# Four changes to the opening of a hybrid attention layer: load order, halved first weights, in-place low parts, deferred stores and rotary splits

## The chip, the cores and the metric

The kernel runs on one core of a Trainium2 chip. A core has five engines that this text speaks of: TensorE (PE in the profile; PEld is its weight load) multiplies matrices, VectorE (DVE) and ScalarE (ACT) work elementwise, GpSimd (POOL) does the same more slowly, and SyncE (SP) here issues every transfer, in one queue. Each engine works through its own list of instructions in order; between engines stand semaphores. The metric is device time in microseconds (us), lower is better.

## The reference

One layer of a decoder: 16 learned meta tokens and 2048 tokens x of width 1024, normalised by RMS and a gain, go through one large projection, then through two attentions side by side, stick-breaking attention with 8 heads and sliding-window attention with 16 query heads, 2 key heads, rotary positions and a sink. Both are gated, projected, merged and added to x.

```python
xn = rms_norm(h, norm_gain[l])
proj = xn @ w_in[l]
sb_q, sb_k, sb_v, sw_q, sw_k, sw_v, sb_z, sw_z, g_sb, g_sw = jnp.split(proj, offsets, axis=-1)
o_sb = stick_breaking_attention(sb_q, sb_k, sb_v, valid)      # heads of 64, no rope
q, k = rope(sw_q, pos), rope(sw_k, pos)
o_sw = sliding_window_sink_attention(q, k, sw_v, attn_sinks[l], valid)
y_sb = (o_sb * jax.nn.silu(sb_z)) @ w_branch_sb[l]
y_sw = (o_sw * jax.nn.silu(sw_z)) @ w_branch_swa[l]
merged = jax.nn.sigmoid(g_sb) * y_sb + jax.nn.sigmoid(g_sw) * y_sw
h = h + merged @ w_out[l]
```

The reshapes to heads are left out here. The result is normalised once more.

## The kernel before

Every product of float32 matrices is made of three matmuls. An operand is split into a high part h (rounded to the multiplier's format) and a low part l = operand - h, and h·h, l·h and h·l are summed in one PSUM bank (`gemm`, L404 to L406). A *tile* here is one such product of 128 output columns with a *group* of 512 tokens: 8 steps over the 1024 inputs, 24 matmuls. There are four groups; a half of the work takes two of them, the first half groups 2 and 3 (g0 and g1 below).

A weight block of 1024 x 128 is loaded (`load`), split by `weights` and `split` (L104: the cast to h on ScalarE or GpSimd, the difference on VectorE or GpSimd, as the flags `hsplit` and `vsplit` say), and both parts are stored to memory, since the second half loads them again. In the opening these stores are not issued at once but collected in `put_off`. Weight parts have three buffers, raw blocks two. Temporaries of 128 x 512 come from one ring of seven buffers (`tmp`): whoever asks for one waits until the last reader of its former content is done, and that reader may be a transfer.

The opening (L900 to L1036) works on unnormalised x, so that TensorE need not wait for the norm: x times gain is split into `xh`/`xl` (`unscaled`, L911 and L912), three products per group are made (stick-breaking keys and queries of the first two head pairs: `ts[0]` keys, `ts[1]` queries, `ts[2]` keys), and their sums are scaled by 1/rms afterwards (`scaled`, L934). Meanwhile ScalarE squares the rows of x for the norms, `rb0` and `rb1` spread the scales, and `normal` (L377 to L380) makes the normalised x of each group, with ScalarE and VectorE working on two of its eight tiles in turn. What is done with a sum stands in `use`: for keys and queries `evac_split` (L113, L114) makes two parts in two new temporaries, and four transfers store them (`sb_k`, `sb_q`).

After it the first half's sliding-window part begins (L1055): the key, value and first query block with g0 (`wk`, `wv`, `wq`), the same key and value block with g1, then the second query block, then the stick-breaking values, where attention sets in as a side stream woven into the projections. For rotary positions (`rope`, L595) ScalarE copies four quarters crosswise, VectorE makes two products with cos and sin tables, GpSimd adds; the sum is split at once into keys (`put_k`, L610 and L612: four casts, four differences) or queries (L657, L658). Small work after a tile (transposing values to rows, meta keys) is queued in `pending`, `soon`, `late` and is run inside a later tile (`lagged`, after its second, fourth, sixth step), so that it stands between matmuls on TensorE. The meta keys of the two stick-breaking blocks go through memory: `ms` is stored to `msd` (L1018), and `later` in `sb_k` loads and transposes it, queued by way of `held`. The buffers `ms` are two.

The order of TensorE is written out by hand everywhere; that of ScalarE and SyncE in the opening too, that of VectorE from there to the value tile of g1 (`hand.close()`). Elsewhere a planner orders the instructions by a simulated timeline and so also decides which buffer is free first.

Of the kernel before, what the change touches and what calls it, by code (L numbers as in the profile page):

```python
# [44 lines left out]
def tile_kernel(ctx, tc, x, xt, meta, metat, gain, w_in, w_sb, w_sw, w_out, sinks, fgain,  # L45
# [18 lines left out]

    A.preload_act_table_set("natural_log_exp_and_others")
    ident = cp.tile([P, P], F32, name="ident")
    DMA(ident, ident_c)
    gn = cp.tile([P, KT], F32, name="gn")
    DMA(gn, gain.rearrange("o (k p) -> p (o k)", p=P))
    sel = cp.tile([P, 2, P], I32, name="sel")  # L70
    skb = cp.tile([P, 16], F32, name="skb")

# [88 lines left out]
        DMA(raw, w[c0 // P])  # L161
        return raw

    def weights(c0, w=w_in, raw=None):
# [265 lines left out]
    def col_tile(w, g, use, first=False, bank="g", mbank="zm"):  # L430
# [4 lines left out]
        use(g, acc, None if pm is None else meta_sum(pm))  # L435
        yield 0.65

    def sb_k(p):
        def use(g, acc, ms):
            h, l = tmp(F32R), tmp(F32R)  # L440
            evac_split(h, l, acc)
            for i, t in enumerate((h, l)):
                DMA(kd[p][g][i][:, :GT], t)
            if ms is not None:
                def later():
                    if p < 2:
                        t = tp.tile([NM, P], F32, tag="ms", name="ms", bufs=2)
                        DMA(t, msd[p])
                    mc = meta_cols(t if p < 2 else ms, "t" if p < 2 else "zm")
                    h, l = tmp(F32R)[:, :NM], tmp(F32R)[:, :NM]  # L450
                    A.copy(h, mc)
                    V.tensor_tensor(l, mc, f32(h), op=ALU.subtract)
                    for i, t in enumerate((h, l)):
                        DMA(kd[p][3][i][:, GT:], t)
                pending.append(later)
        return weights(C_SBK + p * P), use, True

    def sb_q(p):
        def use(g, acc, ms):
            h, l = tmp(F32R), tmp(F32R)  # L460
# [108 lines left out]
    def lagged(gen):  # L569

        for n, c in enumerate(gen):
            yield c
            if n in (2, 4, 6):
                flush({2: soon, 4: late, 6: pending}[n])


    def window(half, groups, sp):
        kk = sp.tile([P, 4, 9 * P], F32R, name="kk")
# [38 lines left out]
        def sw_k():  # L617
            def use(g, acc, ms):
                n = g - groups[0]
                t = tmp()  # L620
                rope(acc, ct[:, cols(n)], sn[:, cols(n)], t, tmp(), 1.0)
                put_k(t, n * GT, GT)
                if ms is not None:
                    def later():
                        t, u = (tmp()[:, :NM] for _ in range(2))
# [22 lines left out]
        def sw_q(p):  # L648
            def use(g, acc, ms):
# [4 lines left out]
                for a in range(2):  # L654
                    r = slice(64 * a, 64 * a + 64)
                    o = slice(64 - 64 * a, 128 - 64 * a)
                    A.copy(q[r, a, :], t[r])  # L657
                    V.tensor_tensor(q[o, a, :], t[r], f32(q[r, a, :]), op=ALU.subtract)  # L658
                qs[p, g] = q, clock[0] + QW
            return weights(C_SWQ + p * P), use, False  # L660

# [240 lines left out]
    with (tc.tile_pool(name="start", bufs=1, side="left") as bp,  # L902
# [39 lines left out]
        ssq0, ssq1 = sums(), sums()  # L942
        for t in (ssq0, ssq1):
            V.memset(t, 0.0)
        ts = [sbt[0]()]
        x_tiles(("u", g0), 1)
        for k in range(KT):
            raws.append(bp.tile([P, GT], F32, tag="raw0", name="raw0", bufs=KT))
            unscaled(g0, k, raws[k])
        ts.append(sbt[2]())  # L950
        ssm = squares(meta, NM, 1)
        ts.append(sbt[1]())
        products(g0, 0, "g")
# [61 lines left out]
        for k in (4, 5):  # L1015
            new.append(pair[:, (k - 4) * GT:(k - 3) * GT])
            DMA(new[k], xt[g1, k])
        for n in (0, 2):  # L1018
            DMA(msd[n // 2], ms[n])
        for k, t in put_off:  # L1020
            DMA(k, t)
        del put_off[:]
        ready[C_SWQ] = weights(C_SWQ, raw=raw)
        outs[g0, 2] = scaled(g0, 2, rb0)
        for n in range(3):
            ts[n][1](g0, outs[g0, n], ms[n])
        for n in range(3):
            outs[g1, n] = scaled(g1, n, rb1)
        for k, t in put_off:
            DMA(k, t)  # L1030
        for k in range(0, KT, 2):
            in_turns(*(normal(g1, j, new[j], rb1) for j in (k, k + 1)))
            if k == 0:
                for j in (6, 7):
                    new.append(ring_x())
                    DMA(new[j], xt[g1, j])  # L1036
    put_off = None
    held = pending[:]
    del pending[:]
    for half, groups in enumerate(halves):  # L1040
        with tc.tile_pool(name=f"swa{half}", bufs=1, side="left") as sp:
# [12 lines left out]
            steps = [(s, g) for s in range(4) for g in groups]  # L1054
            if m:  # L1055
                (wk, use_k, _), (wv, use_v, _), (wq, use_q, _) = sw_k(), sw_v(), sw_q(0)
                drain(col_tile(wk, g0, use_k), col_tile(wv, g0, use_v), col_tile(wq, g0, use_q, bank="z"))
                for n in range(3):
                    ts[n][1](g1, outs[g1, n], None)
                drain(lagged(col_tile(wk, g1, use_k, True, "o", "t")))  # L1060
                meta_k = pending[:]
                del pending[:]
# [101 lines left out]
```

## Time and profile before

| what | value |
|---|---|
| time, median of 3 runs | 2207.05 us (2206.35 to 2208.54) |
| the profiled execution | 2209.05 us, its span 2207.3 us |
| TensorE busy | 2160.9 us (98%) |
| VectorE, ScalarE, GpSimd busy | 1365.7, 1013.8, 380.2 us |
| mean granted TensorE clock | 0.994 |
| bytes moved by DMA | 384.61 MB, mean 174 GB/s |

The span is from the first instruction to the last. A row of a timeline has the start, the length, the engine, the line, the operation with output and input, and in brackets how long the engine had stood idle before it and what ended that wait. A row of the waits has the total, the number of times and the longest. SPq is SyncE's issue of a transfer, not the transfer. Matmuls are pipelined, so one may be listed with 0.39 us though the next starts 0.23 us later.

### The profile page before, as it was taken

The numbers are of one execution on the slowest core, as the hardware profiler recorded it, in microseconds if no ns is written. First come the engines' busy times: TensorE is split into PE (matmuls) and PEld (weight loads), VectorE is DVE, ScalarE is ACT, GpSimd is POOL, SyncE is SP. The second block draws the span as 40 slices with busy tenths as digits, with TensorE's granted clock in tenths as the row PEclk, the third lists the DMA queues.
The fourth block names the chain that finished last, engine by engine and source line by source line (L and its number), as shares of the span: only waits on it lengthen the run. The fifth ranks groups of instructions, "written<-read, shape, count | busy, mean of one in ns | idle before, by whom it ended". The sixth has DMA issues, their size and how long they took to land.

```text
span 2207.3 us, 30283 instructions
## 1 busy us (share of the span) xinstructions
PE 2160.9 (98%) x10614; PEld 1771.3 (80%) x10614; DVE 1365.7 (62%) x2130; ACT 1013.8 (46%) x2332; POOL 380.2 (17%) x493
## 2 busy tenths in 40 slices
PE   8899999999999999999999999999999999999998
PEld 6678887788888888788887888888888888787876
DVE  6678876356555443778755888778774437453543
ACT  6566767333433323677753555555553202221121
POOL 2123342322222201233310000000000232000000
PEclk9999999999999999999999999999999999999999
DMA  9655446856455365544446433333323976467422
GB/s 335 232 175 189 172 171 210 261 182 203 161 179 180 130 232 181 172 172 151 155 135 196 120 110 113 116 99 112 115 84 129 348 271 212 147 221 271 151 91 86
DMA packets 175800, 384.61 MB, mean 174 GB/s; under 512 B 23040, under 2 KB 41216, under 8 KB 175648
## 3 DMA queue, kind: packets, MB, share of 16 engines
q1 hardware_dynamic: 175648, 382.67, 52.0%
q8 instruction: 84, 1.38, 0.3%
q14 instruction: 68, 0.56, 0.1%
HBM read 233.16 MB, written 149.37 MB: 173 GB/s over the span
## 4 chain that ended last, share of the span: by engine, by line
PE 77%; issue 2%; DVE 1%; DMA 1%; ACT 1%; POOL 0%; POOLq 0%; ACTq 0%; DVEq 0%
PE ps_g L404 12%; PE ps_g L405 12%; PE ps_g L406 12%; PE ps_o L861 6%; PE ps_z L813 6%; PE ps_t L835 5%; PE ps_o L722 1%; PE ps_z L676 1%; PE ps_g L224 1%; PE ps_g L225 1%; PE ps_z L225 1%; PE ps_g L223 1%; PE ps_z L223 1%; PE ps_z L224 1%; PE ps_t L225 1%
## 5 line engine op out<-in xcount | busy, mean ns | idle before, releaser
L404 PE MATMUL ps_g<-xh,wh 128*128 128x512 f32 x1544 | 639.2, 414 | 9.7 <-ACT xh L911 7.5
L405 PE MATMUL ps_g<-xl,wh 128*128 128x512 f32 x1544 | 609.2, 395 | 0.4 <-DVE xl L912 0.4
L406 PE MATMUL ps_g<-xh,wl 128*128 128x512 f32 x1544 | 608.9, 394 | 0.0
L824 DVE TENSOR_TENSOR_SCAN row<-row 128x512 f32<-128x512 f32 (+2 forms) x320 | 372.5, 1166 | 176.4 <-POOL row L822 105.1
L406 PEld LDWEIGHTS ps_g<-xh,wl 128*128 128x128 f32 x1544 | 291.7, 189 | 65.5
L404 PEld LDWEIGHTS ps_g<-xh,wh 128*128 128x128 f32 x1544 | 293.4, 190 | 57.3 <-ACT xh L911 7.5
L405 PEld LDWEIGHTS ps_g<-xl,wh 128*128 128x128 f32 x1544 | 293.2, 190 | 43.9 <-DVE xl L912 0.9
L817 ACT ACTIVATE row<-ps_z 128x512 f32<-128x512 f32 (+1 forms) x320 | 172.0, 538 | 276.2 <-PE ps_z L813 228.7
L114 DVE SCALAR_TENSOR_TENSOR wtl<-ps_t,wth 128x512 fp32r<-128x512 f32 (+1 forms) x320 | 189.8, 593 | 42.9 <-ACT wth L113 41.4
L113 ACT ACTIVATE wth<-ps_t 128x512 fp32r<-128x512 f32 (+1 forms) x320 | 170.4, 532 | 97.4 <-PE ps_t L835 95.8
L813 PE MATMUL ps_z<-kt,q 128*128 128x512 f32 (+3 forms) x640 | 185.0, 369 | 0.3 <-ACT row L817 0.3
L835 PE MATMUL ps_t<-ident,row 128*128 128x128 f32 x1088 | 171.6, 273 | 1.2 <-DVE row L824 1.2
L835 PEld LDWEIGHTS ps_t<-ident,row 128*128 128x128 f32 x1088 | 135.9, 140 | 37.3 <-DVE row L824 1.7
L109 POOL TENSOR_SCALAR wh<-raw 128x1024 fp32r<-128x1024 f32 (+1 forms) x71 | 75.8, 1067 | 437.6 <-PE ps_g L405 303.7
L822 POOL TENSOR_SCALAR_AFFINE_SELECT row<-row 128x128 f32<-128x128 f32 x128 | 44.1, 346 | 619.0 <-ACT row L817 584.0
L813 PEld LDWEIGHTS ps_z<-kt,q 128*128 128x128 f32 x640 | 118.7, 188 | 26.4 <-ACT row L817 0.8
L861 PE MATMUL ps_o<-wth,vc 128*128 128x512 f32 (+1 forms) x320 | 125.7, 393 | 1.3 <-DVE tmp L866 1.1
L552 ACT ACTIVATE tmp<-ps_g 128x512 f32<-128x512 f32 x112 | 67.1, 599 | 121.0 <-PE ps_g L406 113.9
L684 ACT ACTIVATE sc<-sc,nm 128x129 f32<-128x129 f32 x256 | 100.0, 392 | 37.0 <-DVE nm L682 36.4
L861 PE MATMUL ps_o<-wtl,vc 128*128 128x512 f32 (+1 forms) x320 | 116.8, 365 | 0.0
L110 POOL TENSOR_TENSOR wl<-raw,wh 128x1024 fp32r<-128x1024 f32 (+1 forms) x43 | 96.4, 2242 | 3.1
L262 ACT CAST ringl<-gt 128x512 fp32r<-128x512 f32 x32 | 19.9, 621 | 132.0 <-DVE gt L260 128.0
(293 smaller groups left out, 3457.8 us busy)
## 6 DMA issues: line engine op xcount, KB each, us to landing
raw<-in_w_in SPq DMA_DIRECT2D x58, 512.0 KB, 4.5
h_in_w_in<-wh SPq DMA_DIRECT2D x58, 512.0 KB, 3.2
l_in_w_in<-wl SPq DMA_DIRECT2D x58, 512.0 KB, 3.4
wh<-h_in_w_in SPq DMA_DIRECT2D x58, 512.0 KB, 3.7
wl<-l_in_w_in SPq DMA_DIRECT2D x58, 512.0 KB, 4.8
q<-qd SPq DMA_DIRECT2D x128, 128.0 KB, 3.4
vc<-vd SPq DMA_DIRECT2D x48, 256.0 KB, 2.7
kd<-tmp SPq DMA_DIRECT2D x32, 256.0 KB, 4.1
```

Of the source, the lines that this page charges most:

```text
L110: (V if vsplit[0] else G).tensor_tensor(l, src, f32(h), op=ALU.subtract)
L113: A.activation(h, acc, AF.Copy, scale=scale)
L114: V.scalar_tensor_tensor(l, acc, scale, f32(h), op0=ALU.mult, op1=ALU.subtract)
L404: T.matmul(acc, lhsT=wh[:, k, :], rhs=xh[g][:, k, :], start=k == 0, stop=False)
L405: T.matmul(acc, lhsT=wh[:, k, :], rhs=xl[g][:, k, :], start=False, stop=False)
L406: T.matmul(acc, lhsT=wl[:, k, :], rhs=xh[g][:, k, :], start=False, stop=k == KT - 1)
L684: A.activation(sc[:, hh, :], sc[:, hh, :], AF.Exp, bias=nm[:, hh:hh + 1], accum_out=den[:, hh:hh + 1])
L813: T.matmul(z[:, :w], lhsT=lq, rhs=kt[h][:, k0:k0 + w], start=t == 0, stop=t == 1)
L817: A.activation(r[:, :w], z[:, :w], AF.Sigmoid, scale=-1.0)
L824: V.tensor_tensor_scan(r[:, :w], r[:, :w], r[:, :w], last[j] if n else 1.0, op0=ALU.mult, op1=ALU.min)
L835: T.transpose(tr[:, j * P:(j + 1) * P], rows_of[h, g, n - (j > i), j][:, k0:k0 + P], ident)
L861: T.matmul(o[:, :n], lhsT=v, rhs=r, start=first and r is wh, stop=last and r is wl)
```

## The change

Four edits, all in the opening and the first tiles behind it.

- *Load order and halves.* The first weight block is loaded ahead of everything, the gain vector behind it, the identity behind the second weight block. The first block is split by halves (steps 0 to 3, then 4 to 7): the first half on ScalarE and VectorE, the second after the first x tile, on ScalarE and GpSimd.
- *Low parts over the sums.* While `spare` is set, `sb_k` and `sb_q` write the low part into the temporary that holds the sum.
- *Stores behind the last x.* The stores of the sliding-window weights (`put_off`: key, value and first query block, two parts each) and of `msd` are issued behind the loads of g1's last two x tiles, no longer ahead of the first group's key and query stores. The second group's sums are split and stored ahead of its normalised x, no longer among the rotary products.
- *Rotary products ahead of their splits.* For the first three tiles (`hold`), `put_k` and the query split are kept in `waiting` and run after all three ropes. `held` is queued one round later.

```diff
-    DMA(ident, ident_c)
     gn = cp.tile([P, KT], F32, name="gn")
-    DMA(gn, gain.rearrange("o (k p) -> p (o k)", p=P))
...
+    spare = [False]
+    def low(acc):
+        return acc.bitcast(F32R) if spare[0] else tmp(F32R)
...                                   # sb_k and sb_q, each
-            h, l = tmp(F32R), tmp(F32R)
+            h, l = tmp(F32R), low(acc)
...
+    waiting = []
+    def then(f):
+        if hold[0]:
+            waiting.append(f)
+        else:
+            f()
+    hold = [False]
...                                   # sw_k
-                put_k(t, n * GT, GT)
+                then(lambda: put_k(t, n * GT, GT))
...                                   # sw_q: the split becomes put_q
+                then(put_q)
...                                   # opening
+        def by_halves(wh, wl, raw):
+            a, b = slice(0, KT // 2), slice(KT // 2, KT)
+            A.copy(wh[:, a], raw[:, a])
+            V.tensor_tensor(wl[:, a], raw[:, a], f32(wh[:, a]), op=ALU.subtract)
+            def rest():
+                A.copy(wh[:, b], raw[:, b])
+                G.tensor_tensor(wl[:, b], raw[:, b], f32(wh[:, b]), op=ALU.subtract)
+            second.append(rest)
+        raw = load(C_SBK)
+        DMA(gn, gain.rearrange("o (k p) -> p (o k)", p=P))
+        ready[C_SBK] = weights(C_SBK, raw=raw, split=by_halves)
         ts = [sbt[0]()]
         x_tiles(("u", g0), 1)
         for k in range(KT):
             raws.append(bp.tile([P, GT], F32, tag="raw0", name="raw0", bufs=KT))
             unscaled(g0, k, raws[k])
+            if k == 0:
+                second[0]()
         ts.append(sbt[2]())
+        DMA(ident, ident_c)
...
-        for n in (0, 2):
-            DMA(msd[n // 2], ms[n])
-        for k, t in put_off:
-            DMA(k, t)
-        del put_off[:]
         ready[C_SWQ] = weights(C_SWQ, raw=raw)
+        spare[0] = True
         outs[g0, 2] = scaled(g0, 2, rb0)
         for n in range(3):
             ts[n][1](g0, outs[g0, n], ms[n])
         for n in range(3):
             outs[g1, n] = scaled(g1, n, rb1)
-        for k, t in put_off:
-            DMA(k, t)
+        for n in range(3):
+            ts[n][1](g1, outs[g1, n], None)
+        spare[0] = False
+        for n in (0, 2):
+            DMA(msd[n // 2], ms[n])
         for k in range(0, KT, 2):
             in_turns(*(normal(g1, j, new[j], rb1) for j in (k, k + 1)))
             if k == 0:
                 for j in (6, 7):
                     new.append(ring_x())
                     DMA(new[j], xt[g1, j])
+                for j, t in put_off:
+                    DMA(j, t)
...                                   # first half
+                hold[0] = True
                 drain(col_tile(wk, g0, use_k), col_tile(wv, g0, use_v), col_tile(wq, g0, use_q, bank="z"))
-                for n in range(3):
-                    ts[n][1](g1, outs[g1, n], None)
+                hold[0] = False
+                flush(waiting)
                 drain(lagged(col_tile(wk, g1, use_k, True, "o", "t")))
...
-                pending.extend(held)
+                pending.append(lambda: pending.extend(held))
```

More of the change, by code (lines that the diff above doesn't have):

```diff
@@ L162, in load, with weights @@
         return raw
-    def weights(c0, w=w_in, raw=None):
+    def weights(c0, w=w_in, raw=None, split=split):
         if c0 in ready:
@@ L459, in use @@
         def use(g, acc, ms):
-            h, l = tmp(F32R), tmp(F32R)
+            h, l = tmp(F32R), low(acc)
             evac_split(h, l, acc, 0.125)
@@ L653, in use, with put_q @@
                 q = sp.tile([P, 2, GT], F32R, tag="q", name="q", bufs=QB)
[L654 to L658, printed above, removed]
+                def put_q():
+                    for a in range(2):
+                        r = slice(64 * a, 64 * a + 64)
+                        o = slice(64 - 64 * a, 128 - 64 * a)
+                        A.copy(q[r, a, :], t[r])
+                        V.tensor_tensor(q[o, a, :], t[r], f32(q[r, a, :]), op=ALU.subtract)
+                then(put_q)
                 qs[p, g] = q, clock[0] + QW
@@ L944, in tile_kernel @@
             V.memset(t, 0.0)
+        second = []
+        def by_halves(wh, wl, raw):
[9 more added lines that the diff above has]
+        ready[C_SBK] = weights(C_SBK, raw=raw, split=by_halves)
         ts = [sbt[0]()]
```

## The prediction

> **What bounds the kernel now.** I read the page's shares first, then TensorE's waits over the opening, then busy time and granted clock by stretch.
>
> ```profile
> PE 2160.9 (98%) x10614; PEld 1771.3 (80%) x10614; DVE 1365.7 (62%) x2130; ACT 1013.8 (46%) x2332; POOL 380.2 (17%) x493
> ```
> ```profile
> PE ps_g L404 <- ACT xh L911: 7.5, 1, 7.5
> PE ps_zm L473 <- ACT tmp L469: 3.7, 1, 3.7
> PE ps_zm L520 <- DVE vt L114: 3.0, 2, 1.6
> PE ps_o L405 <- DVE xl L380: 2.7, 3, 2.2
> PE ps_o L404 <- ACT xh L378: 2.4, 3, 1.3
> PE ps_t L427 <- DMA ms<-msd: 1.9, 1, 1.9
> ```
> ```profile
> 47.10:112.80 65.70, 55.07 (x252) 42.45 (x249) 39.30 (x64) 31.65 (x63) 16.37 (x17) 0.92 0.66 231
> 74.68:78.09 3.41, 3.41 (x15) 2.63 (x16) 1.80 (x3) 3.33 (x6) 1.28 (x1) 0.52 0.80 261
> 95.16:98.58 3.42, 3.42 (x10) 2.65 (x9) 3.25 (x5) 3.26 (x7) 0.12 (x1) 0.52 0.73 216
> 105.41:108.82 3.41, 3.41 (x21) 2.93 (x19) 1.51 (x6) 1.11 (x4) 0.00 (x0) 0.52 0.04 5
> 112.80:160.00 47.20, 44.10 (x238) 36.51 (x238) 37.18 (x74) 32.45 (x97) 13.96 (x16) 1.00 0.57 190
> 160.00:2190.00 2030.00, 2012.48 (x9903) 1653.07 (x9902) 1249.17 (x1912) 913.82 (x2100) 343.59 (x450) 1.00 0.51 169
> ```
>
> In the last fence each row is a stretch: its length, then busy time and instructions of TensorE, its weight loads, VectorE, ScalarE and GpSimd, the granted clock, and the transfer engines' share and rate. TensorE is busy 98% of the span, and the built order of instructions differs from the old one only up to the first tiles of attention. So the change can move only what TensorE loses there: the start (7.5 us), and the stretch from 47.10 to 112.80, in which it stands idle 65.70 - 55.07 = 10.6 us and runs three times for 3.41 us at half the clock (0.52), which costs another 0.48 x 3.41 = 1.6 us each.
>
> **Part 1, the opening loads and the halves.** These rows are SyncE's issues, the first work of ScalarE and VectorE and TensorE's first wait for it, and then TensorE in full run: three matmuls, one step of a product, take 0.68 us.
>
> ```profile
> 1.71 0.58 SPq L55 DMA_DIRECT2D raw<-in_w_in  x1
> 2.33 3.99 SPq L55 DMA_DIRECT2D raw<-in_xt  x8
> 6.65 0.33 SPq L55 DMA_DIRECT2D raw<-in_w_in  x1
> 5.65 1.04 ACT L107 CAST wh<-raw 128x1024 fp32r<-128x1024 f32 x1 [3.59 <-DMA raw<-in_w_in]
> 6.73 1.22 DVE L110 TENSOR_TENSOR wl<-raw,wh 128x1024 fp32r<-128x1024 f32 x1 [4.31 <-ACT wh L107]
> 8.67 0.79 PE L405 MATMUL ps_g<-xl,wh 128*128 128x512 f32 x1 [0.37 <-DVE xl L912]
> ```
> ```profile
> 52.66 0.39 PE L404 MATMUL ps_g<-xh,wh 128*128 128x512 f32 x1
> ...
> 53.34 0.39 PE L404 MATMUL ps_g<-xh,wh 128*128 128x512 f32 x1
> ```
>
> The weights are issued first, ahead of two others, by at most the 1.71 us at which they are issued now and nearer to 0.9. The gain vector stays ahead of the first x tile, which must not land later. That tile landed at about 6.6 (the issue at 6.65 waits for it), just as the cast ended (5.65 + 1.04); so an earlier, halved cast alone gains little, and the gain is the x tile's: 0 to 0.9 us, since it still queues behind the weights and the gain's 4-byte pieces. I take 0.8 and start TensorE at 6.7. VectorE's half (1.22/2 = 0.6) now ends before x, so the second matmul no longer waits for it. Against that stand the second cast of 0.5 us, ahead of the next x tiles on ScalarE, and its difference on GpSimd, beside VectorE's own work. The first matmuls run at half rate in either case, so an earlier start is partly spent there: of 0.8 to 1.2 us I keep **0.5** (bounds: a loss of 0.5, a gain of 1.2).
>
> [...]
>
> **Part 2, what runs into the second group's first tile.** SyncE's queue, VectorE, ScalarE, and the stores' usual time to landing.
>
> ```profile
> 50.72 1.19 SPq L55 DMA_DIRECT2D l_in_w_in<-wl  x1
> 52.02 3.17 SPq L55 DMA_DIRECT2D kd<-tmp  x2
> ```
> ```profile
> 50.66 0.69 DVE L934 TENSOR_TENSOR tmp<-ps_z,rb 128x512 f32<-128x512 f32 x1
> 58.62 0.69 DVE L934 TENSOR_TENSOR tmp<-ps_o,rb 128x512 f32<-128x512 f32 x1 [7.27 <-DMA kd<-tmp]
> ...
> 63.00 1.29 DVE L380 TENSOR_TENSOR xl<-xs,xh 128x512 fp32r<-128x512 f32 x2 [1.67 <-ACT xh L378]
> ```
> ```profile
> 59.93 0.59 ACT L598 ACTIVATE tmp<-ps_g 32x512 f32<-32x512 f32 x1 [10.04 <-DMA qd<-tmp]
> ```
> ```profile
> kd<-tmp SPq DMA_DIRECT2D x8, 256.0 KB, 4.1
> ```
>
> VectorE stands 7.27 us for a temporary buffer that the store of the first group's keys holds, and that store queues behind the weights' (four of 0.5 MB, of which 50.72 is the last). Now the weights' six stores go last, and the low parts reuse the sums. The store leaves at about 48.4 (with the first high part) and lands, by its row's 4.1 us, at 52.5. Then come two sums, to 53.9. Three high parts (0.63 each) that wait for one landing each are ready by 55.6, and with the last low part (0.69) the moved products are done at 56.3. The rope copies of ScalarE follow (4 x 0.6, to 58.0). So the first pair of x tiles has its high parts at 59.2, and low parts at 59.2 and 59.9 instead of 63.7 and 64.3; each later pair takes 2.7 (four VectorE operations of 0.67), so the eighth low part stands at 68. TensorE is at that tile after three others of 8 steps from 47.10, at 63.8 - 0.5 = 63.3, and needs the eighth low part at the end of its eighth step, 7 x 0.69 + 0.2 later, at 68.3. Of the 2.7 + 2.4 = 5.1 us I give back 0.4: **-4.7** (bounds 2.5 and 5.1; the poor end is a landing of 6.6 us, from 52.02 to 58.62, as now). The last two x tiles are issued behind six stores of keys and queries, at about 60.2, and have to land by 65.3: 1.6 MB of stores from about 57 and 0.5 MB of tiles at 0.33 MB per us (261 GB/s at a share of 0.80, in the row from 74.68) end at 63.4, and a landing follows by a us or two.
>
> **Part 3, the collision of VectorE and GpSimd.** The last two x tiles' products were slow for another reason than their loads.
>
> ```profile
> 69.05 1.55 POOL L109 TENSOR_SCALAR wh<-raw 128x1024 fp32r<-128x1024 f32 x1 [14.78 <-DMA xs<-in_xt]
> 70.69 2.67 POOL L110 TENSOR_TENSOR wl<-raw,wh 128x1024 fp32r<-128x1024 f32 x1
> ```
> ```profile
> 71.06 2.84 DVE L377 SCALAR_TENSOR_TENSOR xs<-xs,gn,rb 128x512 f32<-128x512 f32 x1
> ```
>
> An operation that takes 0.7 us elsewhere took 2.84 while GpSimd split the second query weights. After the change that split uses the buffers of the key weights, so it waits until TensorE has left them and those weights' stores have landed, and stands behind both rope additions: cast at about 71, split until 75.5 to 76. TensorE asks for it at 77: a tile is 8 x 0.69 = 5.5, a meta product 16 matmuls of a quarter of the columns, by estimate 0.9, and 63.3 + 5.5 + 0.9 + 5.5 + 0.9 with the transposes is 76.6. The split then meets the key splits of VectorE (L612) instead of the x tiles. The next weights' low part (1.22, as at 6.73; the value projection's) stands behind these on VectorE, and comes at 82 to 85, where TensorE, one tile further, asks at about 83. I take **+1.0** (bounds 0 and 2.6).
>
> [...]
>
> **Part 4, rotary products, value transposes and meta keys.**
>
> ```profile
> 81.71 0.63 ACT L113 ACTIVATE tmp<-tmp 128x512 fp32r<-128x512 f32 x1
> ...
> 89.61 0.63 ACT L113 ACTIVATE tmp<-tmp 128x512 fp32r<-128x512 f32 x1 [0.95 <-DVE tmp L114]
> ...
> 93.32 0.59 ACT L469 COPY tmp<-ps_z 128x512 f32<-128x512 f32 x1 [0.77 <-DMA qd<-tmp]
> ...
> 112.91 0.17 ACT L530 COPY tmp<-ps_zm 128x16 f32<-128x16 f32 x1 [5.63 <-PE ps_zm L427]
> ```
>
> Three splits of the second group (0.63 each on ScalarE, the first at 81.71, the last at 89.61) and their waits leave the way of the copy at 93.32. After the last x tile's cast at 67.3 ScalarE has one copy (0.6), rope of q (4 x 0.6), a split (0.6), rope of k (2.4), four key casts and two q casts (0.63 each, as the splits), and then that copy, done at about 78 with small ones between; TensorE wants it in the seventh step of its tile from 76.6, at 81.5. **-3.7**, with +0.5 for the bank in which it lands, which VectorE empties only after the deferred splits. Deferring costs on: the second group's key splits, the value rows and the next rope stand behind GpSimd's addition, so the 16-column transposes of the meta keys and the product after them may wait, on a path that is quiet now: **+1.0** (0 to 2).
>
> The wait of 1.9 us for the reload of the meta keys stays. The second reload uses the first one's buffer, so it is issued only after the first transpose, and in the new order the two transposes still stand side by side; moving them one tile later hides the first load alone: 0. After it ScalarE waits 5.63 us for TensorE, so the lag of the other engines ends there, and what is won should stay won: from 160 on TensorE is 99% busy at full clock.
>
> **The sum.** Idle time and new waits: -0.5 - 4.7 - 3.7 + 0.5 + 1.0 + 1.0 = -6.4. Two of the three stretches at half clock (the first two, each right after a stall that goes) fall away: -3.2; the third stays with that 1.9 us. Six restarts after short stalls go with them; no row prices them alone, and between 0 and 0.3 us each I take 0.15: -0.9. In all **-10.5 us**. The profiled execution took 2209.05 us (its span and 1.75 around it), which gives 2198.5; the median of the runs shown, 2207.05, lies 2.0 below it, which gives 2196.5. I say 2197.5.
>
> **The rivals.** A measurement of this kernel tells 0.2%, 4.4 us.
> - *All of it.* No new wait shows, and the third half-clock stretch goes too: 2197.5 - 2.5 - 1.6 - 0.4 = 2193. For it: the new waits are of 1 us and stand on estimates. Against: GpSimd's collision is in the trace. 0.17.
> - *The temporaries still wait for stores.* Each landing takes 6.6 us instead of 4.1, and the chain of six such waits ends 3 to 4 us later; the x tiles come late by as much, and half clock with them: 2202. For it: 58.62 - 52.02. Against: 2 MB less in front. 0.15.
> - *Won and lost again.* The attention that follows is bound by ScalarE or VectorE, not by TensorE's arrival: 2207. Against: 5.63 us of ScalarE's waiting at 112.9. 0.07.
> - *Slower: the late weight stores hold GpSimd.* The second query weights need the key weights' buffers, whose stores (0.5 MB each) now go after everything else; GpSimd stands in order, with the rope of q behind it. I reckon that they land at 68. From a landing at about 74, each us later is a us of TensorE; to undo 10.5 they must land at 85, and at 90 the time is 2212. For it: 1 to 3 MB in one queue. Against: the queue moves 0.2 to 0.4 MB per us and is near empty at 105 (5 GB/s). 0.06.
>
> **How the numbers follow.** Forecast 0.55, rivals 0.17, 0.15, 0.07, 0.06. Low end 2190 (all of it, with 3 us more from the start and the clock), high end 2204 (the second rival and a bit): that leaves out the last two and little else. The likeliest case's own range is 2194 to 2201. Faster by over 0.2% means below 2202.6: 0.55 + 0.17 and most of the second rival, 0.85; within: 0.08; slower: 0.07.
>
> **What would show it.** Right: TensorE's first matmul at 6.3 to 7.0; no 7 us wait of VectorE at 51; the waits for x parts (5.1) under 1.5 in all; none for the value copy (3.7); about 1.9 still at the meta transposes; ScalarE's copy of 112.91 at 100 to 104. Wrong: a TensorE wait for the second query weights of GpSimd, for the value weights' low part, or for the keys' rope over 2 us each, or a stall at 63 to 69 as large as now.

## The result, and the profile after

The changed kernel takes 2197.55 us (median of 7 runs, 2194.74 to 2201.59), the kernel before 2207.05 us (7 runs, 2204.25 to 2211.18). The ratio is 0.9955 with a 95% interval of 0.9943 to 0.9968, so the change wins 9.5 us, 7 to 12.6 by the interval; the forecast was 2197.5. The profiled execution took 2194.74 us, its span 2193.0.

Of the changed kernel, first the row of the engines on the page, then TensorE's waits over the first 170 us.

```profile
PE 2153.9 (98%) x10614; PEld 1766.6 (81%) x10614; DVE 1368.2 (62%) x2130; ACT 1014.1 (46%) x2333; POOL 380.7 (17%) x494
```
```profile
PE ps_g L402 <- ACT xh L929: 6.9, 1, 6.9
PE ps_zm L524 <- DVE vt L112: 2.9, 2, 1.6
PE ps_zm L425 <- DVE vv L112: 2.3, 1, 2.3
PE ps_t L425 <- DMA ms<-msd: 1.7, 1, 1.7
PE ps_g L404 <- DVE wl L108: 0.6, 1, 0.6
PE ps_o L403 <- DVE xl L378: 0.2, 1, 0.2
PE ps_t L540 <- DVE tmp L509: 0.2, 1, 0.2
PE ps_o L402 <- ACT xh L376: 0.2, 1, 0.2
```

The waits for the x parts (2.7 and 2.4 before) are down to 0.4, and the 3.7 for the value copy are gone. New are 2.3 us until VectorE has made the value rows' low part (`vv`) out of the bank `zm`, and 0.6 for a weight's low part. The reload of the meta keys keeps its wait, 1.7.

A good place to compare the two is the transpose of meta sums that stands right behind the two reloaded ones; behind it the order of TensorE is the same. Call it the mark. Before and after:

```profile
112.64 0.23 PE L427 MATMUL ps_zm<-ident,ms 16*128 16x16 f32 x1
```
```profile
102.35 0.21 PE L425 MATMUL ps_zm<-ident,ms 16*128 16x16 f32 x1
```

It comes 10.3 us earlier. The stretches of the changed kernel, with the granted clock as the number before the last two:

```profile
47.10:102.50 55.40, 50.29 (x250) 39.84 (x248) 39.99 (x63) 31.32 (x62) 16.61 (x17) 0.97 0.77 274
91.21:94.62 3.41, 3.41 (x12) 2.52 (x12) 2.76 (x5) 1.58 (x7) 1.28 (x1) 0.50 1.02 416
102.50:149.70 47.20, 44.12 (x238) 36.53 (x238) 37.36 (x75) 32.64 (x98) 14.11 (x16) 1.00 0.58 191
149.70:2176.00 2026.30, 2009.62 (x9904) 1651.20 (x9903) 1251.27 (x1912) 914.41 (x2101) 343.69 (x450) 1.00 0.51 169
```

TensorE is idle 5.1 us in the first row where it had been 10.6, with one stretch at half clock where there were three. The work behind, 102.50 to 149.70, has the same 47.2 us and 44.1 busy as its counterpart before: what was won stayed won.

| term, in us | forecast | measured to the mark |
|---|---|---|
| opening | -0.5 | -0.4 (start 7.50 to 6.90; the matmul at 16.88 comes at 16.45) |
| x tiles of the second group | -4.7 | -4.7 (5.1 to 0.4) |
| value copy and its bank | -3.2 | -3.6 (3.7 to 0.1) |
| low part of the value weights | +1.0 | +0.6 |
| value rows ahead of the meta transposes | +1.0 | +2.3 |
| reload of the meta keys | 0 | -0.2 |
| half clock | -3.2 | -3.3 (three windows to one, 0.48 x 3.41 each) |
| restarts | -0.9 | -1.0 (what is left) |
| sum | -10.5 | -10.3 |

The two profiled spans lie further apart, 14.3 us. Of the rest, 3.3 us are two windows at half clock that the execution before had later on (four behind the mark against two), in a part of the program that the change leaves alone; the last section comes back to them.

### The profile page after: what moved, and what is told of

Read it like the earlier page. It is cut to its first block, busy times and chain, and to the rows that moved or that the text cites. A ratio compares the mean times of both kernels' runs of the same rounds, so it can differ in the third digit from the quotient of the medians.

```text
span 2193.0 us, 30281 instructions
## 1 busy us (share of the span) xinstructions
PE 2153.9 (98%) x10614; PEld 1766.6 (81%) x10614; DVE 1368.2 (62%) x2130; ACT 1014.1 (46%) x2333; POOL 380.7 (17%) x494
## 4 chain that ended last, share of the span: by engine, by line
PE 86%; DMA 4%; DVE 4%; ACT 3%; issue 2%; SPq 1%; POOL 0%; DVEq 0%; ACTq 0%; POOLq 0%
PE ps_g L402 15%; PE ps_g L403 14%; PE ps_g L404 14%; PE ps_o L879 6%; PE ps_z L831 6%; PE ps_t L853 5%; PE ps_o L740 3%; PE ps_z L694 3%; PE ps_t L723 1%; PE ps_g L223 1%; PE ps_g L222 1%; PE ps_g L221 1%; PE ps_z L223 1%; PE ps_z L221 1%; PE ps_z L222 1%
```

## The experiments

All medians are to be read against 2206.3 to 2207.6 us, which the kernel before took beside each of them. Each interval reaches about 2.8 us to either side, so by an estimate from that (2.8 times the root of two) two of these kernels are told apart by their times alone only from some 4 us on; the verdicts rest on TensorE's waits as well. "Idle" is TensorE's idle time between its first matmul and the mark, and "half" the number of windows of 3.41 us at half clock that the waiting up to the mark set off; in B, E and F one of them runs behind the mark. In K, L and M the transpose that is the mark stands between the two reloaded ones. The later queueing of `held`, a part of the change, was not undone by itself.

| kernel | median | ratio (95%) | idle | half |
|---|---|---|---|---|
| changed | 2197.55 | 0.9955 (0.9943 to 0.9968) | 5.1 | 1 |
| A stores back | 2202.52 | 0.9977 (0.9967 to 0.9987) | 8.2 | 2 |
| B low parts in their own buffers | 2199.45 | 0.9958 (0.9946 to 0.9970) | 6.5 | 1 |
| C no deferral | 2197.00 | 0.9952 (0.9940 to 0.9964) | 7.2 | 2 |
| D banded splits back | 2192.94 | 0.9936 (0.9922 to 0.9950) | 4.5 | 0 |
| E C and D | 2200.58 | 0.9969 (0.9957 to 0.9981) | 7.8 | 4 |
| F old opening | 2198.42 | 0.9956 (0.9944 to 0.9968) | 5.6 | 1 |
| G split on VectorE | 2193.73 | 0.9940 (0.9928 to 0.9952) | 5.0 | 0 |
| H value rows first | 2196.92 | 0.9953 (0.9941 to 0.9965) | 5.0 | 1 |
| J D, reload into temporaries | 2197.41 | 0.9949 (0.9937 to 0.9961) | 6.3 | 1 |
| K D, meta transposes apart | 2191.85 | 0.9935 (0.9923 to 0.9947) | 2.9 | 1 |
| L D, K and H's order | 2194.07 | 0.9944 (0.9930 to 0.9959) | 3.9 | 1 |
| M K and another bank | 2188.71 | 0.9915 (0.9901 to 0.9928) | 1.7 | 0 |

### A and B: is it the order of the stores, or the number of temporaries?

A puts the stores of the weights and of `msd` back to their old place:

```diff
+        for n in (0, 2):
+            DMA(msd[n // 2], ms[n])
+        for k, t in put_off:
+            DMA(k, t)
+        del put_off[:]
         ready[C_SWQ] = weights(C_SWQ, raw=raw)
...
         for n in range(3):
             outs[g1, n] = scaled(g1, n, rb1)
+        for k, t in put_off:
+            DMA(k, t)
...
-                for j, t in put_off:
-                    DMA(j, t)
```

> The changed kernel with the stores of the first weights and of the meta sums back at their old place in SyncE's queue, ahead of the stores of the keys and queries of the two groups; the low parts still go over the sums. Theory (the queue holds the temporaries): the first store of keys again lands at about 58.6 and not at about 53, so VectorE's wait of 1.20 us before the sum at 52.04 grows to 6 or 7 us, the first x tiles' high parts come at about 64 and not at 58.83, and TensorE loses 4 to 6 us at the x tiles of the second group and a stretch at half clock besides: 2203 to 2206. Rival (the number of temporaries decides, the order of the stores does not): TensorE's waits at the x tiles stay under 1 us in all, 2197 to 2199.

VectorE's wait for a temporary, first in the changed kernel, then in A:

```profile
52.04 0.69 DVE L952 TENSOR_TENSOR tmp<-ps_o,rb 128x512 f32<-128x512 f32 x1 [1.20 <-DMA kd<-tmp]
```
```profile
57.85 0.69 DVE L952 TENSOR_TENSOR tmp<-ps_o,rb 128x512 f32<-128x512 f32 x1 [7.35 <-DMA kd<-tmp]
```

The old wait of 7.3 us is back, and TensorE waits 5.5 us for x parts. Its waits in A over the first 110 us:

```profile
PE ps_o L403 <- DVE xl L378: 3.5, 3, 3.0
PE ps_o L402 <- ACT xh L376: 2.0, 3, 0.9
```

The time is 5 us above the changed kernel, half a microsecond under what the theory gave. The queue theory holds: a store of keys behind 2 MB of weight stores keeps its temporary 6 us longer (7.35 us of waiting against 1.20). B:

```diff
-        return acc.bitcast(F32R) if spare[0] else tmp(F32R)
+        return tmp(F32R)
```

> The changed kernel with the low parts of the banded keys and queries in buffers of their own again, the order of the stores as changed. The six sums, six high parts and six low parts then take 18 temporaries of a ring of 7, and not 12, so nearly one more round of the ring waits for landings of about 5 us (a store issued at 49.53 landed at 54.49). Theory (temporaries and queue both count): the first x tile's parts come 4 to 5 us later than at 58.83, TensorE waits 3 to 5 us at the x tiles, and with a half-clock stretch the time is 2201 to 2205. Rival (the order of the stores alone did it): waits at the x tiles under 1 us, 2197 to 2199.

Both theories missed by a little: the waits at the x tiles are 1.4 us, more than the rival's 1 and less than half of the theory's 3 to 5, and the time cannot be told from that of the changed kernel. By the waits, 5.5 us without the new order and 1.4 without the low parts, the order of the stores carries most of this step.

### C, D and E: what freed the value copy?

C switches the deferral off. D moves the second group's banded splits back behind the first three products of attention. E does both, which leaves of the change the opening, the stores and the low parts.

```diff
-                hold[0] = True
+                hold[0] = False
```
```diff
-        for n in range(3):
-            ts[n][1](g1, outs[g1, n], None)
         spare[0] = False
...
                 hold[0] = False
+                spare[0] = True
+                for n in range(3):
+                    ts[n][1](g1, outs[g1, n], None)
+                spare[0] = False
                 flush(waiting)
```

> The changed kernel without the deferral: the key and query splits of the first tiles follow their rotary sums at once. Theory (deferring is what costs the new wait): the 2.30 us for the value rows' low part at 90.52 go, since the key splits of VectorE (5.18 us at 75.08) then run ahead of GpSimd's split of the second query weights (74.45 to 76.85) and take about 2.6, and a half-clock stretch goes with it: 2193 to 2195. Rival (the deferral keeps the copy of the value tile early): ScalarE has 2.5 us more of key casts ahead of the second rotary sum and the copy at 78.29 comes at 80.5 to 82, TensorE waits 1 to 2 us for it, and what follows is no better: 2199 to 2201.

> The changed kernel with the splits of the second group's banded products back behind the first three tiles of attention's products; stores, in-place low parts and deferral as changed. Theory (my part 4): three splits of ScalarE (0.63 each) and the three of VectorE stand again ahead of the copy of the value tile, at 78.29 now, and the stores' landings ahead of its buffer; TensorE waits 2 to 4 us for that copy, and with a half-clock stretch the time is 2200 to 2204. Rival (only the two causes at the x tiles mattered): the wait for the copy stays under 1 us, and the 0.4 us at the x tiles goes: 2196 to 2198.

> The kernel with the second group's banded splits back behind the attention products (the third step of the change undone), and without the deferral of the key and query splits as well, so that only the opening, the order of the stores and the low parts over the sums are left of the change. Theory (these three carry the whole gain; the deferral is worth nothing): 2191 to 2195, as with the deferral (2192.9). Rival (the deferral pays once the banded splits are out of the way, since it lets the second rotary sum of ScalarE run 2.5 us earlier): TensorE waits 1.5 to 3 us more, for the copy of the value tile or for GpSimd's sums, 2195 to 2198.

TensorE's waits for the value copy and its bank: D's row first, then E's.

```profile
PE ps_zm L477 <- DVE vv L112: 0.8, 1, 0.8
```
```profile
PE ps_zm L477 <- ACT tmp L473: 4.1, 1, 4.1
```

With both steps the wait is 0.1, with the move alone (C) 1.7, with the deferral alone (D) 0.8, with neither (E) 4.1, about as in the kernel before. So either step takes most of it. The forecast named the three banded splits as what stands in the way. E's rows show another chain:

```profile
71.01 5.74 DVE L627 TENSOR_TENSOR kk<-tmp,kk 64x512 fp32r<-64x512 f32 x4 [3.15 <-ACT kk L625]
76.78 0.69 DVE L615 SCALAR_TENSOR_TENSOR tmp<-ps_z,ct 128x512 f32<-128x512 f32 x1
```
```profile
78.22 2.13 POOL L617 TENSOR_TENSOR tmp<-tmp 128x512 f32<-128x512 f32 x1 [2.71 <-DVE tmp L616]
```
```profile
80.39 1.26 ACT L674 CAST q<-tmp 64x512 fp32r<-64x512 f32 x2 [2.78 <-POOL tmp L617]
...
84.89 0.58 ACT L473 COPY tmp<-ps_z 128x512 f32<-128x512 f32 x1
```

Four key splits of VectorE, 5.74 us while GpSimd works on weights (71.33 to 75.51) where four took 2.79 at 86.77 in the changed kernel with GpSimd idle, stand ahead of the second rotary product; GpSimd adds late, ScalarE's query cast waits for that, and the value copy stands behind it in ScalarE's queue, with one banded split and four quarter copies in between. The kernel before has the same links, behind key splits from 79.80 to 83.94:

```profile
83.97 0.69 DVE L600 SCALAR_TENSOR_TENSOR tmp<-ps_z,ct 128x512 f32<-128x512 f32 x1
85.41 1.29 POOL L602 TENSOR_TENSOR tmp<-tmp 128x512 f32<-128x512 f32 x1 [5.38 <-DVE tmp L601]
86.74 1.27 ACT L657 CAST q<-tmp 64x512 fp32r<-64x512 f32 x2 [1.00 <-POOL tmp L602]
```

There two of the banded splits follow the cast, from 88.03 to 90.24, so both causes were in the way. The deferral takes the key splits out of this chain. Where the move is left out it is worth 7.6 us (E to D), though my theory for E gave it nothing and the rival 2 to 5; 3.3 of them are waiting, and E's profile has four windows at half clock that D's has not. Beside the move it is worth nothing that the times show (C, 2197.00). C missed both its forecasts: the 2.3 us for the value rows went, as its theory says, but 1.7 at the bank and 2.0 at the next meta product came.

D also beats the changed kernel's median by 4.6 us, though the intervals overlap a little, against both the theory (2200 to 2204) and its rival (2196 to 2198). Its mark comes at 98.67, 3.7 us earlier, with 0.7 us less idle time and one window at half clock fewer. Without the deferral it is the other way round: there the kernel with the move is 3.6 us faster (E to C), again with intervals that overlap. The trace says how the move costs. SyncE's issue of the last two x tiles, in the changed kernel and in D:

```profile
62.14 1.03 SPq L55 DMA_DIRECT2D xs<-in_xt  x2
```
```profile
57.20 0.93 SPq L55 DMA_DIRECT2D xs<-in_xt  x2
```

The moved splits bring their six stores ahead of these loads. In the six profiles with the move and the new store order (changed, B, C, F, G, H) TensorE waits 0.4, 1.4, 1.9, 0, 1.0 and 1.5 us at the x tiles; in the six without the move (D, E, J, K, L, M) never. And the 2.0 to 2.3 us for the value rows occur only with the move and the deferral together (0.5 in A, none in C).

### F: the opening

The identity and the gain are loaded first again, and the first weights are cast and split whole (the reverse of the diff).

> The changed kernel with the old opening: identity and gain loaded first, the first weights cast and split whole. Theory (my first step): the first matmul starts at 7.4 to 7.6 instead of 6.5 to 6.9 and the second waits another 0.3 to 0.4 us for the low part; by 17 us 0.4 to 0.6 us of it are left, since the first matmuls run at half rate in either case: 2197.7 to 2198.5. Rival (the window at whose end the clock rises, 10.8 to 13.2 us in the runs so far with one and the same opening, decides where TensorE stands at 17 us): no difference in time that follows the start, 2196.5 to 2198.

TensorE starts at 7.47, as expected, and waits another 0.50 for the low part, where 0.3 to 0.4 was expected; with the new opening the starts are 6.5 to 7.3 in twelve profiles. But the clock's rise moves too. The record of the granted clock sets in, at full, at 12.70 us in the changed kernel and at 13.39 in the kernel before, where TensorE's matmuls go from 0.43 us apart to 0.23, and the expectation has 10.8 to 13.2 for one and the same opening. So 2198.42 against 2197.55 tells nothing: half a microsecond is below what a comparison of these kernels resolves. The earlier start is confirmed in the trace; that it shortens the kernel is not shown.

### G and H: where the 2.3 us come from

The value rows' low part in the changed kernel, by engine (VectorE, GpSimd, ScalarE):

```profile
75.08 5.18 DVE L627 TENSOR_TENSOR kk<-tmp,kk 64x512 fp32r<-64x512 f32 x4 [2.02 <-ACT kk L625]
...
89.80 0.67 DVE L112 SCALAR_TENSOR_TENSOR vv<-ps_zm,vv 128x512 fp32r<-128x512 f32 x1
```
```profile
74.45 2.40 POOL L108 TENSOR_TENSOR wl<-raw,wh 128x1024 fp32r<-128x1024 f32 x1
76.82 1.50 POOL L107 TENSOR_SCALAR wh<-raw 128x1024 fp32r<-128x1024 f32 x1
83.93 2.15 POOL L617 TENSOR_TENSOR tmp<-tmp 128x512 f32<-128x512 f32 x1 [5.62 <-issue]
```
```profile
86.11 2.54 ACT L625 CAST kk<-tmp 64x512 fp32r<-64x512 f32 x4 [6.95 <-POOL tmp L617]
88.67 0.60 ACT L111 ACTIVATE vv<-ps_zm 128x512 fp32r<-128x512 f32 x1
```

The key splits take 5.18 us while GpSimd works on weights, where the next four, at 86.77 with GpSimd idle, take 2.79; the next rotary sum is late; the next key casts wait 6.95 us for it; and the value rows stand behind these casts on ScalarE. G takes the collision away, H the order on ScalarE.

```diff
                 hand.close()
-                vsplit[0] = False
```

> The changed kernel with the low part of the second query weights on VectorE (1.22 us, at about 73.1, where VectorE stands idle for 2.02 us) instead of GpSimd (74.45 to 76.85); all else as changed. Theory (the meeting of GpSimd's split and VectorE's key splits is what makes the 2.30 us wait): the four key splits take 2.6 to 3.2 us instead of 5.18, everything behind them on VectorE comes 2 us earlier, the wait for the value rows' low part falls from 2.30 to under 0.8 and that for the value weights from 0.62 to under 0.2, and the half-clock stretch behind goes: 2192 to 2194.5. Rival (VectorE is simply full there, one engine's split is as good as the other's): the waits stay at 2 to 3.5 us, 2197 to 2199.

```diff
-                hold[0] = False
                 flush(waiting)
                 drain(lagged(col_tile(wk, g1, use_k, True, "o", "t")))
+                hold[0] = False
...
                 drain(col_tile(wv, g1, use_v, True, "z", "t"))
+                pending.extend(waiting)
                 hand.close()
+                own = ExitStack()
+                own.enter_context(tc.manual_schedule(engines={mybir.EngineType.Activation}))
...
                 drain(tiles_by_tile(q[0][1:], groups[:1]))
+                own.close()
```

> The changed kernel with the second key tile's splits held back too, until the value rows of that group have been copied, so that on ScalarE the high part of the value rows (at 88.67 in the changed kernel) stands ahead of the four key casts (86.11), which wait 6.95 us for GpSimd's sum. Theory (the 2.30 us wait is ScalarE's order: the value rows' transposes are done at 83.2 and stand behind casts that cannot start before 86.1): the value rows' parts come at 84 to 86, TensorE's wait at 90.52 goes, and with it the half-clock stretch at 91.21: 2193 to 2195. Rival (the path through GpSimd and the key splits ends last anyway): 1.5 to 2.5 us of waiting come back at the meta product or at the next transposes, 2196 to 2198.

G's split and key splits on VectorE, and H's waits of TensorE over the first 110 us:

```profile
74.19 1.21 DVE L108 TENSOR_TENSOR wl<-raw,wh 128x1024 fp32r<-128x1024 f32 x1
76.28 3.68 DVE L627 TENSOR_TENSOR kk<-tmp,kk 64x512 fp32r<-64x512 f32 x4 [0.87 <-ACT kk L625]
```
```profile
PE ps_zm L413 <- DVE tmp L615: 1.8, 1, 1.8
PE ps_t L425 <- DMA ms<-msd: 1.5, 1, 1.5
PE ps_o L402 <- ACT xh L376: 1.3, 1, 1.3
```

In G the key splits are 1.5 us shorter, but VectorE gives 1.2 of it to the split that it has taken over; they end at 79.96 instead of 80.26, and the wait for the value rows is still 2.0. The rival was right about that wait. The 0.6 for the value weights did go, yet the median, 2193.7, lies where the theory put it; idle time of 5.0 us against 5.1 does not carry that, and the window at half clock that its profile lacks in the opening is worth only 1.6 us. I count G as open on the time and as a miss on the mechanism. In H the wait for the value rows is gone, as its theory says, and 1.8 us stand at the next meta product: its rival's case, and its time. There VectorE reads the bank `zm`, in which the meta keys lie, only after other work, and TensorE wants it for the meta product.

### J, K, L and M: the waits that are left

All four build on D, whose waits are 0.8 (value copy), 2.1 (meta product) and 1.5 (reload). J loads the meta keys into temporaries. K puts a tile between the two transposes. L adds H's order. M adds to K that the attention's meta keys are transposed into the bank `o`, which the second key tile has left.

```diff
-                        t = tp.tile([NM, P], F32, tag="ms", name="ms", bufs=2)
+                        t = tmp()[:NM, :P]
```

> The kernel with the second group's banded splits back behind the attention products, and the two reloads of the meta sums into temporaries instead of the two-buffer ring that they share with the sums, so that the second reload need not wait for the first transpose. Theory (the shared buffer makes the wait): the 1.5 us that TensorE waits for the reload between the two transposes go, with 0.15 of restart: 2190.5 to 2192. Rival (the reload moves no earlier, since the temporaries are taken, or something else ends last there): the wait stays at 1 us or more, 2192.5 to 2194.

```diff
-                pending.append(lambda: pending.extend(held))
+                pending.append(lambda: pending.extend([held[0], lambda: pending.append(held[1])]))
```

> The kernel with the second group's banded splits back behind the attention products (2192.9), and the two transposes of the reloaded meta sums one tile apart, so that the second reload, which waits for the first transpose to leave the shared buffer, runs beside a whole tile of products. Theory (a shared buffer between two transposes that stand side by side makes the wait): the 1.5 us wait between them goes and none comes in its place, 2190.5 to 2192. Rival (the second transpose, or what stands behind it, waits as long one tile later): 2192.5 to 2194.5.

> Three edits together: the second group's banded splits back behind the attention products, the two meta transposes one tile apart, and the second key tile's splits behind the value rows (ScalarE in written order over that one tile). Theory (each removes a wait of its own: 1.5 us at the reload, 2.08 us at the meta product, for which VectorE's sum over the meta columns stands behind four key splits that take 3.79 us): 2188 to 2190.5. Rival (VectorE and GpSimd are full from 65 to 95, and what one wait gives another takes): 2191.5 to 2194.

```diff
-                        rope(meta_cols(ms), cm, sm, t, u, 1.0)
+                        rope(meta_cols(ms, "o"), cm, sm, t, u, 1.0)
```

> The kernel with the banded splits back behind the attention products and the two meta transposes apart (2191.85), and one more edit: the meta columns of the attention keys are transposed into the accumulator bank that the second key tile has left, so that the next meta product need not wait until VectorE's rotary sum has read the shared bank behind four key splits. Theory (a bank shared by two short uses makes the 2.07 us wait at the meta product): that wait goes, with 0.15 of restart, and no other grows; a half-clock stretch may go with it: 2188 to 2190. Rival (the meta sums, whose copies stand behind the same work on ScalarE and VectorE, hold TensorE one step later instead): 2191 to 2193.

SyncE's issues in J, and TensorE's waits in M over the first 170 us:

```profile
88.92 0.32 SPq L55 DMA_DIRECT2D tmp<-msd  x1
97.70 0.80 SPq L55 DMA_DIRECT2D kd<-tmp  x2
98.55 0.42 SPq L55 DMA_DIRECT2D tmp<-msd  x1
```
```profile
PE ps_g L402 <- ACT xh L929: 6.9, 1, 6.9
PE ps_zm L524 <- DVE vt L112: 2.8, 2, 1.6
PE ps_zm L477 <- DVE vv L112: 1.4, 1, 1.4
PE ps_t L540 <- DVE tmp L509: 0.3, 1, 0.3
PE ps_t L425 <- DMA ms<-msd: 0.3, 1, 0.3
```

J missed: the second reload stands in SyncE's queue behind the store of the first meta keys' parts, so it leaves at 98.55, after the first transpose, and TensorE's wait grew from 1.5 to 2.8. Another buffer was not enough; the order in the queue held it. K did as its theory says: the wait for the reload is gone and none came in its place. L missed, and its rival was right that what one wait gives another takes: the meta product waits 3.1 us there. M ended that wait by the bank; 0.3 of the reload's wait and 0.6 more at the value copy came back, and no window at half clock is left in the opening. M is faster than both kernels: its interval, 0.9901 to 0.9928, lies wholly below that of the changed kernel. The single steps from D to K and from K to M are too small for the times; they rest on the waits.

## Why the prediction was right, and where it was not

The time was forecast at 2197.5 and came at 2197.55. That it is so near is luck: the forecast lay halfway between two starting points that differed by 2.0 us, and the seven runs spread over 6.9. The sum to the mark, -10.3 against -10.5, holds one miss of +1.3 us, which smaller ones the other way made good.

- **Opening.** The start is right: the first matmul at 6.90 lies in the forecast 6.3 to 7.0, though four of the twelve profiles with this opening start at 7.1 to 7.3. That 0.4 us remain of the 0.5 that I kept is luck in part. The clock rose at 12.70 here and at 13.39 in the kernel before. F, with the old opening, starts 0.57 us later than the changed kernel, and 2198.42 against 2197.55 shows that the time itself cannot tell the step. No run shows the 3 us that the low end allows for the start and the clock; between these two profiles the start moved by 0.60 and the rise by 0.69.
- **The second group's first tile.** Right in cause and size, -4.7. A shows the cause by undoing it. The buffers saved by the low parts count for less than the order (B).
- **The collision.** "The split then meets the key splits of VectorE (L612) instead of the x tiles" is what happened: 5.18 us for four, against 2.79 for the next four. How much key splits are slowed beside that split no run had shown ahead of the result; the +1.0 and its bound of 2.6 were my estimate. I booked it at the value weights' low part (0.6 instead of 1.0) and the "path that is quiet now" separately at 1.0. In the changed kernel they are one chain, and its end, the wait for the value rows, was the mis-sized term: 2.3 instead of 1.0, just outside its bounds of 0 and 2. What makes it is the order on ScalarE, for it goes in H; taking the collision away leaves 2.0 of it (G).
- **The value copy.** The size was right, -3.6, the reason only in part. The step that fell short is "Three splits of the second group" that "leave the way of the copy". Taking them out does shorten the wait (E to C, 4.1 to 1.7), but the deferral does it alone (E to D, 4.1 to 0.8), and it does so at the key splits ahead of the second rotary product, which the forecast did not name. I costed the deferral as a loss only.
- **The move's own price.** I counted the six stores ahead of the last x tiles and let them land in time. They did so with 0.4 us of waiting in this profile, but with up to 1.9 in others. Costed as a gain, the move is one only without the deferral (E to C); beside it, D is the faster kernel. Both comparisons are of medians whose intervals overlap, so the move's own worth stays open; its waits do not.
- **Half clock.** Two windows fewer, as forecast, and the two named did go. But the third went too, for the reload's wait of 1.7 us is followed by none, and a new one, at 91.21, follows the new wait of 2.3 us. The term held because these two errors cancelled, which is luck.
- **Restarts.** No run prices the 0.15 us that I took for each; the -1.0 in the table is what the other terms leave.
- **Where the gain ends.** From the mark to 149.7 nothing was given back, as the forecast argued from ScalarE's idle time.

None of the rivals came true. A is the nearest to one of them: with the stores in the old order the temporaries do wait for the landings, and the time is 2202.5, the 2202 that the rival gave.

## What to carry to other kernels

A store is the last reader of its buffer: what stands ahead of it in the queue decides when that buffer comes free (VectorE waited 7.35 us for one in A, 1.20 in the changed kernel), so loads that are needed and stores that free buffers go ahead of stores that nothing waits for, and a step that brings its own stores ahead of a load can cost even when its arithmetic is free (0 to 1.9 us here). Where a copy is late, follow it back through every queue on its way before naming what holds it; here the cause sat two engines away from the wait. When a wait is left between two short uses of one bank or buffer, give them two or a tile's distance: those of K and M, two lines, and the second group's banded splits in their old place win another 8.8 us on the 9.5 of the change.

## What the runs showed of the chip that I had not expected

Stalls of about 2 us were followed by half clock, and it mattered where they lay. In the changed kernel the three stretches at half clock ahead of the program's end are 3.41 us long and start at 91.21, 364.27 and 1876.38, which is 80 and 443 times 3.413 us apart. Laid out from these starts, two pairs of neighbouring windows of the changed kernel, in the columns of the stretches above:

```profile
87.80:91.21 3.41, 1.11 (x5) 0.62 (x4) 2.61 (x5) 3.30 (x7) 0.00 (x0) 1.00 1.04 417
91.21:94.62 3.41, 3.41 (x12) 2.52 (x12) 2.76 (x5) 1.58 (x7) 1.28 (x1) 0.50 1.02 416
889.87:893.28 3.41, 1.69 (x8) 1.10 (x7) 1.78 (x4) 3.33 (x8) 0.00 (x0) 1.00 0.91 294
893.28:896.70 3.42, 2.82 (x16) 2.17 (x17) 3.42 (x7) 1.46 (x3) 1.59 (x1) 1.00 0.06 18
```

With 2.30 us idle in a window the next ran at half clock; with 1.72 it did not. In the profiles of the kernel before and the changed kernel, both laid out so, and but for the empty windows at the program's end, the eight windows with 2.06 to 2.64 us of idle TensorE are each followed by one at half clock. Of the fourteen with 1.23 to 1.87 us two are, with 1.42 and 1.87, both in the kernel before; none with 1.17 us or less is. By the granted clock of 0.52 and 0.50 a window at half clock costs about 0.48 x 3.41 = 1.6 us, an estimate. The reload's wait came out both ways: in the changed kernel its 1.70 us lay across the end of a window at 101.45, with 0.89 us idle in the window ahead and 0.81 in the one behind, and the clock stayed at 1.00; in the kernel before 1.87 us fell in the window from 102.14 to 105.55, and the next ran at 0.50. Most of the spread of the runs goes with the clock: the seven runs of the changed kernel have mean clocks from 0.997 (2194.74 us) to 0.994 (2201.59 us), and 0.003 of 2195 us are 6.6 of these 6.9 us. Programs that are all but the same behind the mark can differ there too: the kernel before has four windows at half clock behind it (from 375.20, 388.86, 907.68 and 1890.72) and the changed kernel two, without the one in which the program ends.

GpSimd's rotary sum took 2.15 us (at 83.93 in the changed kernel) instead of 1.28 (at 93.18) where VectorE's split of weights (1.21 us at 83.72) had started just before it, and VectorE's four key splits 5.18 instead of 2.79 beside GpSimd's work on weights (74.45 to 78.32). Why the two engines slow each other here was not shown. What I had not expected is G: the split moved to the faster engine (1.21 us there, 2.40 on GpSimd) takes 1.5 us off the key splits and puts 1.2 into that engine's queue.
